# One decoder kernel, its feature mixer: `c` spread by identity products, fewer unread products, two more columns loaded ahead, one engine order into the MLP

## The chip, the cores and the metric

One core of one Trainium2 chip runs the whole program. The metric is the device time in microseconds (us) of one execution; three runs of the kernel before are given, and one more execution was profiled.

## The reference

The reference is a decoder of two layers over 512 tokens of width 1024, all in float32. Layer 0 mixes tokens with a pool mixer, layer 1 with a gated unit; each layer then has an MLP of width 4096 with a squared ReLU. Before every mixer and MLP the activations are normalised, scaled and shifted, and each result is gated; the scales, shifts and gates are `mod = silu(c) @ ada_w + ada_b`, 12288 numbers in all from one vector `c`.

```
c_act = jax.nn.silu(c)
for i in range(DEPTH):
    mod = c_act @ ada_w[i] + ada_b[i]
    sh1, sc1, g1, sh2, sc2, g2 = jnp.split(mod, 6, axis=-1)
    h = modulate(rmsnorm(x, norm_mix_g[i]), sh1, sc1)
    y = pool_mixer(h, ...) if i == 0 else sgu_mixer(h, ...)
    x = x + g1[:, None, :] * y
    h = modulate(rmsnorm(x, norm_mlp_g[i]), sh2, sc2)
    x = x + g2[:, None, :] * jnp.square(jax.nn.relu(h @ mlp_w1[i])) @ mlp_w2[i]
return rmsnorm(x, final_g)
```

The pool mixer takes, in each of four groups of 256 features, the mean over a trailing window of 2, 4, 8 or 16 tokens, subtracts the token itself, and multiplies by a 256x256 matrix.

## The kernel before, in words

**Stages.** The program has a head (layer 0's mixer, about the first 58 us), a sweep (the first 7 of the MLP's 32 column tiles of `w1`, done for all 512 tokens, one 128-row slice `k` of the contraction at a time, eight slices), and then `mlp(0)`, the second mixer and `mlp(1)`. Large products are done as three products of halves: a float32 operand is split into a rounded half `wh` (ScalarE copies it) and a rest `wl` (VectorE subtracts).

**Columns of `mod`.** A *column* is a tile of 128 of `mod`'s numbers, 512 KB of `ada_w`. It is done in one of two ways. On VectorE: one SCALAR_TENSOR_TENSOR over 128x1024 multiplies the tile by `cb`, the vector silu(c) spread over all partitions, and adds up along the row (`column`). On TensorE, for a name that ends in P in `WORK`: eight small products `pt` with silu(c) as the stationary operand, a ScalarE copy `prt`, and one product `pm` with `sel` that adds the four parts (`qm`, `qg`, `qn`). Columns are named `m` (scale and shift of the mixer, group and place), `g` (gate, by 128-feature slice) and `n` (scale and shift of the MLP, by slice `k`).

**`cb`.** `spread_row` loads `c` as a row (`row`, 4 KB), multiplies it by a row of ones in two products of 512 columns (`pc`), and ScalarE copies the result with Silu.

**The order of the head.** Two lists set it. `LOADS` is the order of the transfers on SyncE's queue; its columns go into a ring of 13 slots (three `w4` tiles and five pairs `wh`, `wl`, which the splits use as well), and a load is issued when its slot's last column has been used. `WORK` is the order of the steps, and each step's instructions go to their engines in that order: `sq`, `rms`, `bandr` (squares of tokens, their inverse roots on GpSimd, the window matrix scaled by them), `win` (window products `pq`), `pd` (ScalarE, scale and shift), `pr` (products `po` with `pool_w`), `gf` and `ad` (gate, and VectorE's addition into `xf`), `xt`/`xd` and `bt`/`be` (transposes to features and back), `sm`/`sk`/`ss` (sums of squares), `tot` and `diag` (inverse root of the sums, spread over partitions as `rb`), `hi`/`lo` (split of a sweep weight). `zN` puts N products of `ones` by `ones`, which nothing reads, ahead of the next bank's first product; `SPIN` does it ahead of the sweep.

**The sweep.** For each `k`: VectorE makes `ht`, ScalarE rounds it to `hb`, VectorE subtracts the rest, TensorE does 21 products of 512 columns, and beside them two columns `n` of the next slice and the split of the next weights are done. Columns that `LOADS` does not name are loaded here, into the three `w4` slots alone (`places`). At the slices in `SPILL`, ScalarE issues a transfer of 1 MB that puts half of `x` away to DRAM. The sweep's sums use three banks of the pool `xz` and the four of `ps` (`rb` has the fourth of `xz`).

**Into the MLP.** `mlp(0)` records its instructions and orders them by a cost table. The head's hand order ends with its `with` block, and `mlp` opens another one. The first thing that TensorE does there is the last of the eight columns of `w1`, in `f_run`, in a bank of `ps`.

Of the kernel before, what the change touches and what calls it, by code (L numbers as in the profile page):

```python
# [7 lines left out]
F32 = mybir.dt.float32  # L8
# [6 lines left out]
P = 128  # L15
D = 1024
# [29 lines left out]
def c_g(n, k):  # L46
# [7 lines left out]
    m11 m10 m13 g3 x m12 m33 g2 m31 g7 m30 pw1 m32 m23 m03 pw3 m22 g6 m20 m21 m00 m02 pw2 m01 g5 pw0 g1 g0 g4  # L54
    n01 n00 raw0 n11 raw1
# [3 lines left out]
    z8 rowc z9 z1 m13P qm13 m11 sq2 g3P m10 sq0V edge z9 z7 xt2 sq1V rms0 rms2 xt1 m12 qg3 gf3 sq3V qm10 rms1  # L59
    rms3 qm11 g2 xt3 m33 qm12 fin1 g7 qm33 xd2 qg7 m31 bandr0 xt0 bandr2 xd1 qg2 xd3 gf7 m30 bandr1 qm30 m32  # L60
    qm31 bandr3 xd0 qm32 fin3 win1 win3 m23 gf2 qm23 pd1 pr2 pd3 pr3 ad2 z1 m03P ad3 m22 pr7 qm22 ad7 g6 m20
    bt10 bt11 m21 qg6 qm21 win2 qm20 be10 fin2 gf6 be11 pr6 m00 m02 ad6 qm02 m01 win0 pd2 qm03 qm01 pr4 pr5
    qm00 fin0 g5 qg5 bt31 gf5 sm13 bt30 pd0 ad5 sm11 g1 be31 g0 pr0 qg1 sm12 be30 pr1 sm33 qg0 sm10 sk5 gf0
    ad0 sm30 sm32 g4P sm31 gf1 qg4 ad1 bt01 be01 gf4 ad4 sk4 bt00 be00V sm03 sm02V ss5 sm01V sm00 hi0 s3 ss4
    n01P bt21 tot n00 lo0 be21 bt20 qn00 n11P qn01 z2 diag nf0 qn11 be20
"""

SPIN = 5
EARLY = 2
SPILL = (6, 7)  # L70
# [278 lines left out]
def decoder_kernel(ctx: ExitStack, tc: tile.TileContext, xtok, vecs, rows, fgrow, ada0, ada1, pool_w, w1s, w1, w1f, w1b, w2, w2e, w_v, w_u, w_o, wsT, lnp, bs, out):  # L349
# [3 lines left out]
    ORDERED = {mybir.EngineType.DVE, mybir.EngineType.Activation, mybir.EngineType.SP, mybir.EngineType.Pool}  # L353
# [219 lines left out]

    with (
        tc.tile_pool(name="st", bufs=1) as st,
        tc.tile_pool(name="st2", bufs=2) as st2,
        tc.manual_schedule(engines={mybir.EngineType.DVE, mybir.EngineType.Activation, mybir.EngineType.SP}),
    ):
        row = st.tile([P, D], F32, name="row")
        Y.dma_start(row[0:1], rows[0:1])  # L580


# [69 lines left out]
        def places(name):  # L652

            kind = name.rstrip("0123456789")
            if kind == "n" and int(name[1]) > 1:
                return slots[0:1]
            return [slots[(nslot[0] + j) % len(slots)] for j in range(kind in ("m", "g", "n"))]

        def load(name):
            kind, d = name.rstrip("0123456789"), [int(c) for c in name if c.isdigit()]  # L660
            for j, (pool, tag) in enumerate(places(name)):
# [5 lines left out]
                nslot[0] += kind != "n" or d[0] <= 1  # L667
# [24 lines left out]
        def column(name, out):  # L692
# [132 lines left out]
        wk = {}  # L825
# [71 lines left out]
        def norm_32(k):  # L897
# [5 lines left out]
            rowc=lambda: spread_row(cb, AF.Silu),  # L903
# [15 lines left out]
        for k in range(KD):  # L919
# [54 lines left out]
    def mlp(i, first, extra, last, ending):  # L974
# [3 lines left out]
        with (  # L978
# [45 lines left out]
            def f_run(u, w):  # L1024
                c, f = u
                po = bank("po")
# [419 lines left out]
    mlp(0, first0, ex, gated, ending0)  # L1446

# [184 lines left out]
def _lay_out(inp):  # L1632
# [21 lines left out]
    d["rows"] = f("c")  # L1654
# [48 lines left out]
```

## Time and profile before

| | |
|---|---|
| median of 3 runs | 824.75 us (821.16, 824.84, 824.75) |
| the profiled execution | 825.6 us |
| its span | 823.9 us |
| TensorE (PE) busy | 808.9 us, 98% |
| VectorE (DVE) busy | 689.3 us, 84% |
| ScalarE (ACT) busy | 484.7 us, 59% |
| GpSimd (POOL) busy | 70.4 us, 9% |
| last gate addition of the mixer starts | 50.96 us |
| first `ht` of the sweep starts | 57.97 us |
| first product of the sweep starts | 59.52 us |
| first product of `mlp(0)` starts | 99.08 us |

Rows of the timeline are: start in us, duration in us, engine, line, operation, output<-inputs, shape, count, and in brackets the engine's idle time before it and what ended it. PEld is TensorE's loading of stationary operands. L102 is the helper through which the head's instructions go, L130 the one of `mlp(0)`, so a line number tells little, and the names of tiles do the work. A float32 product shows as two records.

### The profile page before, as it was taken

The page shows a single profiled execution, that of the slowest core. Times are in us where ns is not written, and L with a number is a line of the kernel's source. Part 1 is how long each engine was busy: PE and PEld are TensorE (multiplying, and loading weights), DVE is VectorE, ACT ScalarE, POOL GpSimd, SP SyncE. Part 2 cuts the span into 40 slices and gives each one's busy share as a digit, 9 for nine tenths or more (in the row PEclk, how much of TensorE's full clock was granted, in tenths as well). Part 3 has the DMA queues.
Part 4 walks back from the last instruction along what each step waited for, and adds up shares of the span by engine and source line. Part 5 has one row for each costly group of instructions (what it writes and reads, how often), then busy time and mean ns, then how long its engine had stood idle before and what let it go on. Part 6 is the DMA issues. An engine that isn't in the chain of part 4 may idle for free.

```text
span 823.9 us, 12793 instructions
## 1 busy us (share of the span) xinstructions
PE 808.9 (98%) x4969; PEld 729.9 (89%) x4969; DVE 689.3 (84%) x936; ACT 484.7 (59%) x703; POOL 70.4 (9%) x96
## 2 busy tenths in 40 slices
PE   9999899999999999999999999999999999999996
PEld 7668788999999999888889888989999999999985
DVE  4989878899999999867798967778789988988865
ACT  2576686675766577257333226676766667677522
POOL 3100001010101010001020001000101000111001
PEclk9999999999999999999999999999999999999999
DMA  9969995989988797627856646947888888777402
GB/s 354 411 235 307 364 283 144 271 222 266 228 275 229 247 249 241 200 84 249 277 158 210 220 157 216 325 105 201 192 266 206 258 227 254 186 175 244 140 26 102
DMA packets 43790, 185.47 MB, mean 225 GB/s; under 512 B 4921, under 2 KB 5073, under 8 KB 36434
## 3 DMA queue, kind: packets, MB, share of 16 engines
q1 hardware_dynamic: 35282, 137.72, 46.2%
q0 software_dynamic: 8016, 44.58, 26.9%
q10 hardware_dynamic: 432, 2.36, 0.7%
q8 instruction: 39, 0.64, 0.3%
q14 instruction: 21, 0.17, 0.1%
HBM read 178.34 MB, written 6.30 MB: 224 GB/s over the span
## 4 chain that ended last, share of the span: by engine, by line
PE 86%; DVE 7%; DMA 3%; ACT 2%; issue 1%; POOL 0%; POOLq 0%; DVEq 0%; ACTq 0%
PE po L102 32%; PE pm L130 18%; PE pm L102 17%; PE po L130 15%; DVE ada L102 2%; DVE wl L102 2%; DMA ada<-in_ada 1%; PE px L102 1%; PE pt L102 1%; PE pc L102 1%; DMA raw<-in_w 1%; DVE wh L102 1%; ACT wh L102 1%; PE pq L102 0%; DVE ht L102 0%
## 5 line engine op out<-in xcount | busy, mean ns | idle before, releaser
L102 PE MATMUL po<-hb,wh 128*128 128x256 f32 (+1 forms) x816 | 177.5, 314 | 0.0
L102 PEld LDWEIGHTS po<-hb,wh 128*128 128x128 f32 x816 | 135.1, 191 | 8.5 <-DVE hb L102 0.7
L102 PE MATMUL po<-hb,wl 128*128 128x256 f32 (+1 forms) x408 | 128.8, 316 | 0.7 <-ACT hb L102 0.7
L102 DVE TENSOR_TENSOR wl<-raw,wh 128x1024 fp32r<-128x1024 f32 (+2 forms) x85 | 99.2, 1171 | 26.9 <-ACT wh L102 26.6
L102 ACT ACTIVATE wh<-raw 128x1024 fp32r<-128x1024 f32 (+2 forms) x85 | 85.7, 1017 | 52.8 <-PE pm L102 21.8
L102 PEld LDWEIGHTS po<-hb,wl 128*128 128x128 f32 x408 | 77.9, 191 | 5.6 <-ACT hb L102 1.3
L130 ACT ACTIVATE wh<-raw 128x1024 fp32r<-128x1024 f32 x48 | 50.8, 1060 | 54.4 <-PE pm L130 19.7
L130 PE MATMUL po<-hb,wh 128*128 128x256 f32 (+1 forms) x400 | 78.1, 296 | 0.0
L102 DVE SCALAR_TENSOR_TENSOR ada<-ada,cb 128x1024 f32<-128x1024 f32 x50 | 60.6, 1220 | 12.7 <-DMA ada<-in_ada 7.3
L130 DVE TENSOR_TENSOR wl<-raw,wh 128x1024 fp32r<-128x1024 f32 x48 | 58.5, 1222 | 9.3 <-ACT wh L130 9.0
L130 PEld LDWEIGHTS po<-hb,wh 128*128 128x128 f32 x400 | 63.7, 191 | 2.0
L102 PE MATMUL pm<-wh,oh 128*128 128x512 f32 x188 | 63.8, 357 | 0.0
L130 PE MATMUL pm<-wh,oh 128*128 128x512 f32 x188 | 63.8, 357 | 0.0
L102 PE MATMUL pm<-wh,ol 128*128 128x512 f32 x168 | 63.7, 379 | 0.0
L130 PE MATMUL pm<-wh,ol 128*128 128x512 f32 x168 | 63.7, 379 | 0.0
L130 PE MATMUL pm<-wl,oh 128*128 128x512 f32 x168 | 63.7, 379 | 0.0
L102 PE MATMUL pm<-wl,oh 128*128 128x512 f32 x168 | 63.7, 379 | 0.0
L130 PE MATMUL po<-hb,wl 128*128 128x256 f32 (+1 forms) x201 | 59.4, 296 | 2.0 <-ACT g L130 2.0
L102 PE MATMUL po<-as,wh 128*128 128x256 f32 x288 | 49.0, 275 | 0.0
L102 PEld LDWEIGHTS po<-as,wh 128*128 128x128 f32 x288 | 43.7, 192 | 0.0
L130 PEld LDWEIGHTS po<-hb,wl 128*128 128x128 f32 x201 | 38.4, 191 | 3.4 <-ACT g L130 2.4
L130 PE MATMUL po<-as,wh 128*128 128x256 f32 x240 | 40.8, 275 | 0.0
(275 smaller groups left out, 1886.9 us busy)
## 6 DMA issues: line engine op xcount, KB each, us to landing
ada<-in_ada SPq DMA_DIRECT2D x76, 512.0 KB, 4.6
raw<-in_w1b SPq DMA_DIRECT2D x44, 512.0 KB, 6.2
b<-in_w SPq DMA_DIRECT2D x18, 1024.0 KB, 6.8
bt<-in_w POOLq DMA_DIRECT2D x18, 1024.0 KB, 8.8
raw<-in_w1b POOLq DMA_DIRECT2D x22, 512.0 KB, 6.4
raw<-in_w2e SPq DMA_DIRECT2D x16, 512.0 KB, 3.7
bt<-in_w SPq DMA_DIRECT2D x6, 1024.0 KB, 8.7
b<-in_w POOLq DMA_DIRECT2D x6, 1024.0 KB, 10.4
```

The lines of the kernel that those rows point to most:

```text
L102: return f(*a, **kw)
L130: self.ops.append((name, attr, lambda: f(*a, **kw), out, ins, kw))
```

## The change

`spread_row` no longer loads a row: for each of the eight slices of silu(c), one product with that slice broadcast over 128 columns as the stationary operand and the identity as the moving one. The TensorE columns take the same broadcast in place of the copy `cab`. `WORK` and `LOADS` are other lists: eight TensorE columns (m20 m00 m13 g3 g6 n01 n00 n21) in place of six (m13 g3 m03 g4 n01 n11), the tokens `x` loaded after two columns in place of four, groups 0, 1, 2 summed by token and group 3 by feature, 19 unread products in place of 37, and `n21` and `n10` in the ring's list. `held` marks the ring slots that the sweep's splits take, and a column in `LOADS` takes a ring slot whatever its slice. `SPIN` is 3 in place of 5, `SPILL` is (5, 7) in place of (6, 7). The hand order stays open until `mlp(0)` has been written out, and `mlp(0)`'s first product takes its bank from `xz`.

```diff
 LOADS = """
-    m11 m10 m13 g3 x m12 m33 g2 m31 g7 m30 pw1 m32 m23 m03 pw3 m22 g6 m20 m21 m00 m02 pw2 m01 g5 pw0 g1 g0 g4
-    n01 n00 raw0 n11 raw1
+    m00 m20 x m02 m01 m13 m10 m03 g0 g1 pw0 m12 m11 g2 g3 m23 pw1 m22 m21 m30 pw2 m31 m33 m32 g4 g5 pw3 g6 g7
+    n00 raw0 n01 n21 n11 n10 raw1
 """
 WORK = """
-    z8 rowc z9 z1 m13P qm13 m11 sq2 g3P m10 sq0V edge z9 z7 xt2 sq1V rms0 rms2 xt1 m12 qg3 gf3 sq3V qm10 rms1
+    z5 rowc edge sq0 z2 m20P sq3 z9 z2 xt3 sq2 sq1V rms0 rms2 xd3 m00P xt2 rms3 rms1 m02 bandr0 xd2 z1 m13P
...
-SPIN = 5
+SPIN = 3
-SPILL = (6, 7)
+SPILL = (5, 7)
...
-    ORDERED = {mybir.EngineType.DVE, mybir.EngineType.Activation, mybir.EngineType.SP, mybir.EngineType.Pool}
+    ORDERED = {mybir.EngineType.Pool}
...
+    ordered = ExitStack()
+    ordered.enter_context(tc.manual_schedule(engines={mybir.EngineType.DVE, mybir.EngineType.Activation, mybir.EngineType.SP}))
     with (
         tc.tile_pool(name="st", bufs=1) as st,
         tc.tile_pool(name="st2", bufs=2) as st2,
-        tc.manual_schedule(engines={mybir.EngineType.DVE, mybir.EngineType.Activation, mybir.EngineType.SP}),
     ):
-        row = st.tile([P, D], F32, name="row")
-        Y.dma_start(row[0:1], rows[0:1])
...
-        def spread_row(o, f):
+        def spread_row(o):
             for n in range(2):
                 pc = bank("pc")
-                T.matmul(pc, ones[0:1, :], row[0:1, S * n : S * n + S], start=True, stop=True)
-                A.activation(o[:, S * n : S * n + S], pc, f)
-
-        cab = st.tile([P, KD, 32], F32, name="cab")
-        V.tensor_copy(cab, ca.unsqueeze(2).to_broadcast([P, KD, 32]))
+                for q in range(4):
+                    k = 4 * n + q
+                    T.matmul(pc[:, P * q : P * q + P], ca[:, k : k + 1].to_broadcast([P, P]), ident, start=(q == 0), stop=(q == 3), skip_group_check=True)
+                A.activation(o[:, S * n : S * n + S], pc, AF.Copy)
...
-            if kind == "n" and int(name[1]) > 1:
+            if kind == "n" and name not in LOADS:
                 return slots[0:1]
...
-                T.matmul(pt[q : q + 32], cab[:, k], r[:, k], start=(k < 4), stop=(k >= 4), tile_position=(0, q), skip_group_check=True)
+                T.matmul(pt[q : q + 32], ca[:, k : k + 1].to_broadcast([P, 32]), r[:, k], start=(k < 4), stop=(k >= 4), tile_position=(0, q), skip_group_check=True)
...
+            held[k] = [(tag, len(taken[tag])) for tag in ("wh", "wl")]
+            for tag, _ in held[k]:
+                taken[tag].append(False)
...
+            for tag, n in held[k]:
+                taken[tag][n] = True
...
-                po = bank("po")
+                po = bank("po", xz if i == 0 and u == (0, SWEEP) else None)
...
     mlp(0, first0, ex, gated, ending0)
+    ordered.close()
```

Three places show how the instructions move. The first is VectorE (DVE) at the sweep's last slice: `ht` and `hb` are its operands, `ada,pmv` is the first column of layer 1, and `xf` and `wl<-raw` belong to `mlp(0)`.

```order
 L102 TENSOR_TENSOR wl<-raw,wh 128x896
 L102 SCALAR_TENSOR_TENSOR ht<-xf,scl_92,rb 128x512
-L130 SCALAR_TENSOR_TENSOR ada,pmv<-ada,cb 128x1024
 L102 SCALAR_TENSOR_TENSOR hb<-ht,mods_89,hb 128x512
+L130 SCALAR_TENSOR_TENSOR ada,pmv<-ada,cb 128x1024
 L130 TENSOR_TENSOR xf<-xf 128x4x256
 L130 TENSOR_TENSOR wl<-raw,wh 128x1024 x3
```

The column of layer 1 stood between `ht` and the rest `hb` of the last slice; now it stands behind `hb`.

The second is VectorE in the sweep's second slice (`k` = 1), where the rows `ada,pm` are the columns `n` of the next slice.

```order
 L102 SCALAR_TENSOR_TENSOR ht<-xf,scl_92,rb 128x512
-L102 SCALAR_TENSOR_TENSOR ada,pm_711<-ada,cb 128x1024
+L102 SCALAR_TENSOR_TENSOR ada,pm_628<-ada,cb 128x1024
 L102 SCALAR_TENSOR_TENSOR hb<-ht,mods_89,hb 128x512
-L102 SCALAR_TENSOR_TENSOR ada,pm_711<-ada,cb 128x1024
 L102 TENSOR_TENSOR wl<-raw,wh 128x896
 L102 SCALAR_TENSOR_TENSOR ht<-xf,scl_92,rb 128x512
```

One of its two columns goes (n21, now a TensorE column ahead of the sweep); the other slices keep theirs.

The third is TensorE at the program's start: `pc` is the spread of `c`, `pt` and `pm` are TensorE columns, rows with `ones` as the only input are unread products.

```order
-L102 MATMUL pc<-ones 128x128 x8
-L102 MATMUL pc<-row,ones 128x512 x2
-L102 MATMUL pt<-ones 128x128 x10
-L102 MATMUL pt<-ada,cab 32x128 x8
-L102 MATMUL pm<-sel,prt 128x1
-L102 MATMUL pt<-wh,cab 32x128 x8
-L102 MATMUL px<-ones 128x128 x16
+L102 MATMUL pc<-ones 128x128 x5
+L102 MATMUL pc<-ident,ca 128x128 x8
+L102 MATMUL pt<-ones 128x128 x2
+L102 MATMUL pt<-ada,ca 32x128 x8
+L102 MATMUL px<-ones 128x128 x11
```

Two long one-row products give way to eight of 128 columns, and of the 34 unread products in these rows 18 are left; the transposes `px` of the tokens follow in both.

More of the change, by code (lines that the diff above doesn't have):

```diff
@@ L348, in decoder_kernel @@
 @with_exitstack
-def decoder_kernel(ctx: ExitStack, tc: tile.TileContext, xtok, vecs, rows, fgrow, ada0, ada1, pool_w, w1s, w1, w1f, w1b, w2, w2e, w_v, w_u, w_o, wsT, lnp, bs, out):
+def decoder_kernel(ctx: ExitStack, tc: tile.TileContext, xtok, vecs, fgrow, ada0, ada1, pool_w, w1s, w1, w1f, w1b, w2, w2e, w_v, w_u, w_o, wsT, lnp, bs, out):
     nc = tc.nc
@@ L666, in load @@
                 taken[tag].append(False)
-                nslot[0] += kind != "n" or d[0] <= 1
+                nslot[0] += kind != "n" or name in LOADS
             if kind == "x":
@@ L823, in backed @@
                 V.tensor_copy(o, b)
-        wk = {}
+        wk, held = {}, {}
         pm2 = {}
```

15 lines of the change are left out of this document (7 added, 8 removed).

## The prediction

> **What bounds the kernel now.** I read the chain of waits first, then the stages, then the timeline where a stage left a question. From the start of `mlp(0)` on it is TensorE alone, one group behind the other:
>
> ```profile
> 114.90 5.18 PE pm L130 x25
> 120.08 5.18 PE po L130 x24
> ```
>
> 24 products of 512 columns take 5.18 us, 0.216 each, with nothing between groups, and so it goes on for most of the span. The change touches none of that work, so it can only move the moment at which this stream begins. What lies ahead of it I read by stages, with the busy time of PE, PEld, DVE, ACT and POOL, the granted clock, the DMA engines' share and GB/s:
>
> ```profile
> 20.00:30.00 10.00, 8.96 (x58) 6.99 (x57) 9.33 (x25) 7.36 (x13) 2.73 (x2) 1.00 1.03 408
> 30.00:40.00 10.00, 10.00 (x63) 6.64 (x62) 9.01 (x19) 3.30 (x6) 0.00 (x0) 1.00 1.03 416
> 40.00:50.00 10.00, 9.68 (x52) 5.25 (x50) 9.51 (x21) 7.28 (x24) 0.00 (x0) 1.00 0.98 402
> ```
>
> In the mixer three resources are full at once: TensorE, VectorE, and the DMA engines at some 410 GB/s, so a 512 KB column lands every 1.26 us (0.524 MB by 0.416). Moving work between engines pays there only where all three allow it.
>
> **The mixer**, up to its last gate addition. In the profile it ends at 51.71 (50.96 + 0.75):
>
> ```profile
> 50.96 0.75 DVE L102 SCALAR_TENSOR_TENSOR xf<-po,mg,xf 128x512 f32<-128x512 f32 x1
> ...
> 57.97 0.75 DVE L102 SCALAR_TENSOR_TENSOR ht<-xf,scl,rb 128x512 f32<-128x512 f32 x1 [1.38 <-PE pm L102]
> ```
>
> *Work on VectorE.* Twenty columns become nineteen up to that point, and three whole squares of tokens become one; each is one pass over 1024 elements, about 1.15 from start to start, so 3.45 less. The copy `cab` goes too. *Data.* The list brings the same 24 columns, tokens and `pool_w`, about 30 units of 512 KB, so the last gate lands when it landed before, less one issue slot of SyncE (the row of `c`, 0.37). Before, that column was issued at 35.30, and such columns took 10.0 to land at the median, a little less late in the list, so about 44.5; now 44.1.
>
> ```profile
> 35.30 0.33 SPq L102 DMA_DIRECT2D wl<-in_ada  x1
> ```
>
> ```profile
> wl<-in_ada SPq DMA_DIRECT2D x10, 512.0 KB, 10.0
> ```
>
> The tokens are units 3 to 6 in place of 5 to 8: 2.5 + 0.4 earlier.
>
> ```profile
> L102 SPq DMA_DIRECT2D x<-in_xtok x4: 449/456/478, 3.4 to 5.0; - x4
> ```
>
> ```profile
> DMA to landing us min/median/max: 7.0/7.8/8.6
> ```
>
> Landing ran from 3.4 + 7.0 = 10.4 to about 5.0 + 8.6, and a unit later at the worst, 14.3; now the last token tile is there by about 11.4. *The windows* need the window matrix scaled by four inverse roots. Now ScalarE squares two tiles behind that landing (two passes of about 1.2, to 13.9), GpSimd does four roots, and ScalarE three `bandr` and four `xf` copies behind the last:
>
> ```profile
> 22.07 2.73 POOL L102 TENSOR_TENSOR r<-v,mhalf 128x1 f32<-128x1 f32 x2 [4.25 <-DVE v L102]
> ```
>
> ```profile
> 24.83 0.78 ACT L102 ACTIVATE bandr<-band,r 128x576 f32<-128x576 f32 x1 [0.37 <-POOL r L102]
> 25.51 1.07 ACT L102 ACTIVATE xf<-px 128x512 f32<-128x512 f32 x2
> ```
>
> Before, the last `bandr` ended at 25.6. Now: 13.9 + 4 x 1.15 = 18.5, + 3 x 0.75 + 4 x 0.54 = 22.9. From there I lay out TensorE's stretch from the rows of the same work:
>
> ```profile
> 34.55 1.04 PE L102 MATMUL px<-ident,xf 128*128 128x128 f32 x8
> 35.42 2.08 PE L102 MATMUL pq<-bandr,x 128*128 128x144 f32 x16
> 37.34 1.88 PE L102 MATMUL po<-pd,pw 128*128 128x512 f32 x4
> ```
>
> From start to start a window group takes 1.92 and a `po` pair 1.72. Group 0's last windows end at 23.4; then come three window groups 5.8, eight products 13.8, two TensorE columns with their sums about 1.9, five half transposes about 2.4, and some 0.1 at each of eight changes of producer: 24.7, so the last product ends at 48.1 and the last addition at 48.1 + 0.15 + 0.75 = 49.0. VectorE's own list, followed against the landings, has its next to last pair added by about 45 and the last gate's column done by 46.3, so TensorE is what ends last, no longer VectorE, which trailed the last product by 2.6. **Term: 51.7 to 49.0, -2.7.** Ends: if TensorE were no limit, landing 44.1, one column and two gates with their additions (1.9) give 47.1, -4.6; if the roots come as late as before, 0.
>
> **To `ht`**, the sweep's first, it took 6.26 more (57.97 - 51.71). The same chain of copy, squares, sum, root on GpSimd, `diag` and `rb` stands there. n11 replaces n00 on VectorE and falls into the 1.38 it idled ahead of `ht`; one more copy back (0.69) lies beside the root. TensorE has three columns in place of two between the sums and `rb`, 0.6 more, of which half shows. **Term: +0.3** (0 to +0.9).
>
> **The sweep.** Each slice from the third on is a chain of VectorE alone:
>
> ```profile
> 66.15 0.66 DVE ht L102
> 66.80 0.98 DVE ada L102
> 67.95 0.67 DVE hb L102
> 68.61 1.14 DVE ada L102 x2
> 69.76 1.00 DVE wl L102
> ```
>
> From 66.15 to 70.76 it takes 4.61, while TensorE's 21 products take 21 x 0.216 = 4.53. The column taken out of `k` = 1 is worth 1.15 to VectorE, but not to the sweep: TensorE then becomes the bound. All 168 products need 36.3. Before, from the first at 59.52 to the end of the last at 96.88 it was 37.36:
>
> ```profile
> 90.51 0.74 DVE L102 SCALAR_TENSOR_TENSOR ht<-xf,scl,rb 128x512 f32<-128x512 f32 x1
> 91.17 1.22 DVE L130 SCALAR_TENSOR_TENSOR ada<-ada,cb 128x1024 f32<-128x1024 f32 x1
> 92.31 0.08 DVE L130 DVE_READ_ACCUMULATOR ada<-ada,cb 128x1 f32 x1
> 92.31 0.75 DVE L102 SCALAR_TENSOR_TENSOR hb<-ht,mods,hb 128x512 fp32r<-128x512 f32 x1
> ```
>
> Here layer 1's column delays the last `hb` by 1.14, and it now stands behind. With both edits VectorE reaches the last `ht` about 30.0 (two slices with one column 3.47, five with two 4.61) + 1.2 (the waits for late columns below) after the first, TensorE the last slice 33.5 after it, so only a wait of about 0.3 in the first slice stays. **Term: -0.8** (0 to -1.1).
>
> The columns still come into three slots and still wait for data:
>
> ```profile
> L102 DVE SCALAR_TENSOR_TENSOR ada<-ada,cb 128x1024 f32<-128x1024 f32 x13 | 15.9, 1223 | 1.2 <-DMA ada<-in_ada 1.2
> ```
>
> n20's load now waits for n21's slot, which TensorE reads some 4.4 after the mixer ends, and SyncE's next loads queue behind it; it is wanted some 10 after. A second spill (1 MB, 2.5 us of the DMA engines) also moves into the sweep. Both fall on VectorE's new margin of about 2 over TensorE.
>
> **Into the MLP.** The gap is plain:
>
> ```profile
> 96.45 0.59 PE L102 MATMUL po<-hb,wh 128*128 128x512 f32 x2
> 99.08 0.49 PE L130 MATMUL po<-hb,wl 128*128 128x256 f32 x2 [2.03 <-ACT g L130]
> ```
>
> ```profile
> 96.54 1.06 ACT L130 ACTIVATE wh<-raw 128x1024 fp32r<-128x1024 f32 x1 [2.03 <-DMA raw<-in_w]
> 97.51 1.04 ACT L130 ACTIVATE as<-xf 128x1024 fp32r<-128x1024 f32 x1
> 98.45 1.06 ACT L130 ACTIVATE g<-po 128x512 f32<-128x512 f32 x2
> ```
>
> TensorE waits for a `ps` bank, whose reader `g` stands on ScalarE behind a split that waits for data. With the bank of `rb`, last read by the last `ht`, the wait goes; the weights of the first product are split by about two us before the sweep ends. What is late next is the second column's bank, wanted 5.2 later, and then `p`'s weights:
>
> ```profile
> 106.99 1.22 DVE L130 TENSOR_TENSOR wl<-bt,wh 128x1024 fp32r<-128x1024 f32 x1
> ```
>
> They were ready at 108.2 for a start at 114.9, so 2.2 can be given back and 4 stay. **Term: 99.08 - 96.88 = -2.2** (-1 to -2.2).
>
> **Other edits.** `cb` from identity products is ready earlier, but VectorE's first column now lands only at about 12.7: nothing. The 18 unread products hid in waits: nothing, unless the clock falls (below).
>
> **Sum:** -2.7 + 0.3 - 0.8 - 2.2 = -5.4. The profiled execution took 825.6 (span 823.9, the rest around it), which gives 820.2; the median of the runs shown, 824.75, lies 0.85 lower, so I say 819.4.
>
> **The clock.** Unread products bought clock at the start:
>
> ```profile
> 4.83 3.78 PE L102 MATMUL pc<-row,ones 1*128 1x512 f32 x4
> 8.54 4.43 PE L102 MATMUL pt<-ones 128*128 128x128 f32 x20
> ...
> 14.83 3.84 PE L102 MATMUL px<-ones 128*128 128x128 f32 x32
> ```
>
> The same record takes 0.22 in the second row and 0.12 in the third, while the granted clock reads 1.00 throughout: the array ran at half rate for the first 13 us. In my layout TensorE is about half idle from 12.7 to 21.2, its longest gap 2.4. [...] No row here shows a gap of that kind.
>
> **Rivals.** One row for the last of them:
>
> ```profile
> DVE mg L102 <- PE pm L102: 3.7, 1, 3.7
> ```
>
>  *(a) The clock falls in the thinned stretch* and comes back after the 4.4 us of dense work that the second row above took: half of it is lost, +2.2, 821.6; if the roots are late as well, 823. [...] *(b) Slower: the clock stays at half through the mixer,* since its work comes in pieces. Then the 24.7 us of TensorE's stretch double, and at 844 it is far slower; it turns slower by 0.5% (828.9, so 9.5 to lose) once half rate lasts for over 19 us. Against it: before, the stretch ran at full rate with waits in it. *(c) TensorE is not the mixer's bound,* the pieces overlap better and the landings decide: -4.6 in place of -2.7, 817.5. *(d) The change doesn't do what it says:* a new wait in the mixer (each engine takes its list in order, and before one gate that waited for TensorE held VectorE for 3.7) eats the mixer's term, and the terms behind the mixer stay: 822.
>
> **Chances.** Forecast 0.48 (817.5 to 821.5), (a) 0.15, (b) 0.07, (c) 0.12, (d) 0.18. A measurement of this kernel can tell about 0.5%, 4.1 us, from no change: faster means below 820.6. The forecast's band gives 0.38 of its 0.48 there, (c) all of its 0.12, (d) and (a) some 0.05 of theirs: 0.55. Slower: (b) and a tail of (d), 0.09. The range leaves out (b) and the tail beyond (c): 815.8 to 824.5.
>
> **What would show it.** Right: the last addition near 49, the first `ht` near 55.4, the sweep's products without a gap behind its first slice, `mlp(0)`'s first product right behind the sweep's last, the chain dense from there. Wrong: products `po<-pd` with pairs over 1.72, VectorE waiting for `po` or columns for long in the mixer, columns landing late in the sweep, or a gap of TensorE among the first groups of `mlp(0)` that gives the 2.2 back.

## The result, and the profile after

| | before | changed |
|---|---|---|
| median (20 executions each) | 823.58 us (820.69 to 825.91) | 819.02 us (818.47 to 822.02) |
| the profiled execution | 825.6 us | 821.9 us |
| last gate addition starts | 50.96 | 49.83 |
| first `ht` of the sweep starts | 57.97 | 56.73 |
| first product of the sweep starts | 59.52 | 58.28 |
| first product of `mlp(0)` starts | 99.08 | 94.83 |
| first product of the second mixer starts | 371.16 | 366.82 |
| first `pm` product of `mlp(1)` starts | 558.09 | 554.41 |

The ratio is 0.9954, with a 95% interval of 0.9942 to 0.9965: 4.56 us less by the medians, where 5.4 was forecast. The 824.75 that the forecast started from was the median of three executions; that of twenty is 823.58. The profiled execution is an unlucky one of the changed kernel (821.9, where the median is 819.0), and its profile tells why.

The end of the mixer and the start of the sweep, on VectorE, in the changed kernel:

```profile
49.83 0.75 DVE L102 SCALAR_TENSOR_TENSOR xf<-po,mg,xf 128x512 f32<-128x512 f32 x1 [0.70 <-PE po L102]
...
56.73 0.75 DVE L102 SCALAR_TENSOR_TENSOR ht<-xf,scl,rb 128x512 f32<-128x512 f32 x1 [0.58 <-PE pm L102]
```

VectorE now waits for TensorE ahead of the last addition, as the prediction had it, but the addition comes only 1.13 earlier. From it to the first `ht` little has changed: 6.15 from the addition's end, where it took 6.26. On TensorE, the sweep's first and last products and `mlp(0)`'s first:

```profile
58.28 0.48 PE L102 MATMUL po<-hb,wl 128*128 128x512 f32 x1 [0.78 <-ACT hb L102]
...
94.40 0.59 PE L102 MATMUL po<-hb,wh 128*128 128x512 f32 x2
94.83 0.39 PE L130 MATMUL po<-hb,wl 128*128 128x256 f32 x2
```

The gap of 2.03 is gone: there is no bracket on the last row. From the sweep's first product to its end it is 94.83 - 58.28 = 36.55, where it was 37.36. From the last addition to `mlp(0)`'s first product it takes 45.00 (94.83 - 49.83) where it took 48.12. The chain of waits shows nothing but TensorE from here on:

```profile
58.28 36.71 PE po L102 x168
95.00 15.55 PE po L130 x73
110.55 5.18 PE pm L130 x25
115.73 5.18 PE po L130 x24
```

The lead at the start of the second mixer is 4.34; at the first `pm` of `mlp(1)` it is 3.68. In between lie the same instructions, and they take 187.59 here and 186.93 before; in the experiments below they take 185.9 to 188.0, so these 0.66 are a difference between executions.

**What is new in the mixer.** TensorE from the first products with `pool_w` on, in the same execution:

```profile
23.65 3.70 PE L102 MATMUL po<-pd,pw 128*128 128x512 f32 x8
27.19 0.28 PE L102 MATMUL pm<-sel,prt 128*128 128x1 f32 x2
28.19 0.64 PE L102 MATMUL pt<-wl,ca 128*32 128x128 f32 x16 [0.73 <-DMA wl<-in_ada]
29.22 0.38 PE L102 MATMUL pm<-sel,prt 128*128 128x1 f32 x2 [0.39 <-ACT prt L102]
30.29 1.97 PE L102 MATMUL px<-ident,xf 128*128 128x128 f32 x8 [0.69 <-DVE xf L102]
32.05 4.42 PE L102 MATMUL po<-pd,pw 128*128 128x512 f32 x8
```

Eight records `po<-pd` take 3.70 in the first row and 4.42 in the last; eight `px` take 1.97. Three waits stand between. The windows (busy PE, PEld, DVE, ACT and POOL, granted clock, DMA share, GB/s) show what they led to:

```profile
26.84:30.25 3.41, 1.65 (x22) 1.00 (x20) 3.22 (x10) 1.76 (x4) 0.00 (x0) 1.00 1.01 406
30.00:30.50 0.50, 0.21 (x1) 0.21 (x2) 0.50 (x2) 0.00 (x0) 0.00 (x0) 0.79 1.00 410
33.50:34.00 0.50, 0.50 (x2) 0.19 (x1) 0.29 (x2) 0.00 (x0) 0.00 (x0) 0.80 1.12 442
```

A mean of 0.79 in the second window is 1.00 that becomes 0.50 at 30.29, and 0.80 in the third is 0.50 that becomes 1.00 at 33.70. The clock was halved for 3.41 us, behind a stretch of the same length in which TensorE was busy for 1.65. The early part differs too:

```profile
3.42 3.37 PE L102 MATMUL pc<-ident,ca 128*128 128x128 f32 x16
...
7.74 2.72 PE L102 MATMUL px<-ones 128*128 128x128 f32 x22
```

3.37 for 16 records is half rate (0.21), 2.72 for 22 is full rate (0.12). The full rate is there at about 6.4; in the kernel before, whose unread products still took 0.22 each at 8.54, it came at 12.7.

### The profile page after: what moved, and what is told of

Its sections match the earlier page's. It is cut to its first block, busy times and chain, and to the rows that moved or that the text cites. A ratio compares the mean times of both kernels' runs of the same rounds, so it can differ in the third digit from the quotient of the medians.

```text
span 820.2 us, 12807 instructions
## 1 busy us (share of the span) xinstructions
PE 804.4 (98%) x4977; PEld 727.5 (89%) x4977; DVE 684.4 (83%) x928; ACT 486.6 (59%) x710; POOL 67.9 (8%) x96
## 3 DMA queue, kind: packets, MB, share of 16 engines
q0 software_dynamic: 8016, 44.58, 27.2%
## 4 chain that ended last, share of the span: by engine, by line
PE 80%; DVE 8%; DMA 6%; ACT 3%; issue 1%; SPq 0%; POOL 0%; POOLq 0%; ACTq 0%; DVEq 0%
PE po L102 28%; PE pm L130 18%; PE pm L102 18%; PE po L130 15%; DMA ada<-in_ada 3%; DVE wl L102 2%; DVE ada L102 2%; DMA wh<-in_ada 1%; DVE v L102 1%; ACT wh L102 1%; DMA raw<-in_w_v 1%; DMA raw<-in_w_o 1%; PE px L102 1%; ACT hb L102 1%; PE pq L102 0%
## 5 line engine op out<-in xcount | busy, mean ns | idle before, releaser
L102 PEld LDWEIGHTS po<-hb,wl 128*128 128x128 f32 x408 | 77.9, 191 | 5.9 <-ACT hb L102 1.0
L102 ACT ACTIVATE g<-g 128x512 f32<-128x512 f32 x50 | 31.5, 630 | 14.8 <-DVE g L102 14.1
```

The lines of the kernel that those rows point to most:

```text
L102: return f(*a, **kw)
```

## The experiments

The theory after the result: the handover and the sweep do what was forecast, and the mixer loses about 1.7 to a clock that falls by chance. The rivals: VectorE or the data bounds the mixer whatever the clock does; and, against the prediction's own account, not the lists but the early clock moves the mixer. The table has all medians, with the times that the profile of one execution gives. *Full rate from* is the start of TensorE's first records that follow at 0.11 in place of 0.21; for the one-row products of 512 columns, it is 0.43 in place of 0.85.

| kernel | median, executions | ratio to before, 95% interval | full rate from | last addition | first `ht` | `mlp(0)` |
|---|---|---|---|---|---|---|
| before | 823.58, 20 | | 12.7 | 50.96 | 57.97 | 99.08 |
| changed | 819.02, 20 | 0.9954, 0.9942 to 0.9965 | 6.4 | 49.83 | 56.73 | 94.83 |
| e1, waits filled | 819.15, 9 | 0.9946, 0.9929 to 0.9963 | 5.3 | 47.95 | 54.85 | 92.96 |
| e2, bank of `ps` | 822.44, 12 | 0.9985, 0.9968 to 1.0003 | 5.1 | 47.45 | 54.35 | 94.02 |
| e3, row spread | 819.01, 10 | 0.9948, 0.9930 to 0.9967 | 13.6 | 47.60 | 54.51 | 92.61 |
| e4, before + handover | 820.14, 12 | 0.9963, 0.9944 to 0.9982 | 5.5 | 48.23 | 55.24 | 93.35 |
| e5, before + identity | 821.83, 12 | 0.9982, 0.9966 to 0.9997 | 7.0 | 47.46 | 54.46 | 94.79 |
| e6, before + open order | 823.94, 12 | 1.0008, 0.9991 to 1.0025 | 13.5 | 51.29 | 58.30 | 98.87 |
| e7, before + `xz` bank | 821.65, 12 | 0.9973, 0.9956 to 0.9990 | 13.3 | 51.22 | 58.23 | 96.92 |
| e8, no unread products | 819.24, 7 | 0.9948, 0.9928 to 0.9969 | 16.2 | 47.09 | 53.99 | 93.79 |
| e9, changed, again | 819.53, 12 | 0.9956, 0.9935 to 0.9977 | 5.9 | 47.82 | 54.72 | 92.83 |
| e10, before + both | 819.56, 12 | 0.9948, 0.9929 to 0.9966 | 6.8 | 48.45 | 55.46 | 94.46 |
| e11, fewer unread | 818.64, 10 | 0.9942, 0.9921 to 0.9962 | 8.5 at the latest, then again 18.4 | 48.38 | 55.28 | 93.39 |
| e12, one-row unread | 830.19, 7 | 1.0085, 1.0058 to 1.0111 | 28.5 | 57.16 | 64.19 | 104.76 |

e1 to e4, e5 to e8 and e9 to e12 ran on one chip each, with the kernel before beside them (medians 823.97, 823.81 and 823.49).

**e1, the waits filled.** In the changed kernel's `WORK`:

```diff
-... qg2 qm20 g3P gf0 ad0 qg3 m23 qm23 bt01 bt00 gf3
+... qg2 qm20 z3 g3P gf0 ad0 z1 qg3 m23 qm23 z3 bt01 bt00 gf3
```

> Changed kernel, plus seven unread products in the three waits of TensorE between 27.2 and 30.3 us (three ahead of g3's products, one ahead of its sum, three ahead of the back transposes). Theory, the clock: the granted clock of 0.50 that the changed kernel shows from 30.2 to 33.7 comes from these waits and costs 1.75; here it stays 1.00, the eight records of po<-pd behind it take about 3.6 in place of 4.42, the last gate addition starts near 48.3 to 48.6 in place of 49.83, and the time falls by 1.2 to 1.5 against the changed kernel's 819.0. Rival, VectorE: the clock stays 1.00, but VectorE, which has no wait from 36.5 to 47.4, sets the end; last addition not before 49.5, time within 0.4 of 819.0. Rival, the waits are not the cause: the clock falls all the same.

VectorE's last addition:

```profile
47.95 0.75 DVE L102 SCALAR_TENSOR_TENSOR xf<-po,mg,xf 128x512 f32<-128x512 f32 x1 [0.69 <-PE po L102]
```

The clock stays at 1.00 and the addition is 1.9 earlier than in the changed kernel's first profile, but the median is the same. The nine executions only spread less: 818.78 to 820.22, where the changed kernel's twenty had 818.47 to 822.02. So what was removed is not in the typical execution.

**e2, `mlp(0)`'s first bank from `ps` again.**

```diff
-                po = bank("po", xz if i == 0 and u == (0, SWEEP) else None)
+                po = bank("po")
```

> Changed kernel with mlp(0)'s first product in a bank of ps again, as before. Theory: TensorE waits for the first g on ScalarE, which starts at 96.6 and ends at 97.1, while the sweep's last product is over at 95.0: a gap of 2.0 to 2.3 ahead of mlp(0)'s first product, and 821.0 to 821.3 in place of 819.0. Rival: the open order already moved g ahead, or the slack behind gives the gap back: gap under 0.5 or time within 0.5 of 819.0.

TensorE's first product of `mlp(0)`:

```profile
94.02 0.49 PE L130 MATMUL po<-hb,wl 128*128 128x256 f32 x2 [1.39 <-ACT g L130]
```

The wait for `g` comes back, shorter in this execution than expected. The median is 3.4 above the changed kernel, more than the gap explains, and the executions spread from 819.75 to 825.55. A part of that spread is told by e6.

The same execution answers a question of e1: it has the changed kernel's mixer, no filled waits, a granted clock of 1.00 all through the mixer, and its last addition at 47.45.

**e3, `c` spread from a row again.**

```diff
-                for q in range(4):
-                    k = 4 * n + q
-                    T.matmul(pc[:, P * q : P * q + P], ca[:, k : k + 1].to_broadcast([P, P]), ident, ...)
-                A.activation(o[:, S * n : S * n + S], pc, AF.Copy)
+                T.matmul(pc, ones[0:1, :], row[0:1, S * n : S * n + S], start=True, stop=True)
+                A.activation(o[:, S * n : S * n + S], pc, f)
```

> Changed kernel with c spread again from a loaded row by two one-row products of 512 columns. Theory of the prediction (other edits: nothing): within 0.5 of 819.0, since VectorE's first column stands at 14.05 and cb would be there by about 9.5. Rival, the early clock: the changed kernel's records of unread and identity products fall from 0.21 to 0.11 apart at 6.4 us, those of the kernel before only at 12.7, behind the one-row products; with the row spread TensorE stays at half rate to about 12.7, the transposes of the tokens end 2 to 3 later, the windows start near 21 to 22 in place of 18.85, and the time rises by 1 to 3.

TensorE's unread products ahead of the transposes, and VectorE's last addition:

```profile
9.43 4.72 PE L102 MATMUL px<-ones 128*128 128x128 f32 x22
```

```profile
47.60 0.75 DVE L102 SCALAR_TENSOR_TENSOR xf<-po,mg,xf 128x512 f32<-128x512 f32 x1 [0.69 <-PE po L102]
```

Both sides had a half of it right. TensorE is at half rate to 13.6 (4.72 for 22 records, where the changed kernel took 2.72), and it costs nothing: the windows start 1.3 later than in the changed kernel's profile (20.18 against 18.85), and the end of the mixer is the same as in e2 (47.60 against 47.45). In the changed order the early clock is not on the path: ahead of the windows VectorE waits for data, ScalarE and GpSimd, and not for TensorE.

**e4, the handover alone.** The kernel before with:

```diff
+    ordered = ExitStack()
+    ordered.enter_context(tc.manual_schedule(engines={...DVE, ...Activation, ...SP}))
...
-                po = bank("po")
+                po = bank("po", xz if i == 0 and u == (0, SWEEP) else None)
...
     mlp(0, first0, ex, gated, ending0)
+    ordered.close()
```

> Kernel before with two edits alone: the hand order stays open through mlp(0), and mlp(0)'s first product takes its bank from xz. Theory: the gap of 2.03 ahead of mlp(0)'s first product goes and the last hb of the sweep is 1.1 earlier: first product of mlp(0) at 96.3 to 96.9 in place of 99.08, time 2.2 to 2.8 below the kernel before. Rival: the handover's wait is for the split that waits for data, and stays: under 0.6 below the kernel before.

On TensorE the one-row products, the sweep's first and `mlp(0)`'s first product, and on VectorE the last addition:

```profile
4.83 2.13 PE L102 MATMUL pc<-row,ones 1*128 1x512 f32 x4
...
56.80 0.48 PE L102 MATMUL po<-hb,wl 128*128 128x512 f32 x1 [0.34 <-ACT hb L102]
...
93.35 0.38 PE L130 MATMUL po<-hb,wl 128*128 128x256 f32 x2
```

```profile
48.23 0.75 DVE L102 SCALAR_TENSOR_TENSOR xf<-po,mg,xf 128x512 f32<-128x512 f32 x1
```

By the medians it is 3.8 less than the kernel before beside it, where 2.2 to 2.8 were expected. From the last addition to `mlp(0)` it takes 45.12, against 48.12 before and 45.00 in the changed kernel: the two edits give all of the handover and the sweep. The sweep takes 36.55 from its first product, as in the changed kernel, although this kernel still does two columns at `k` = 1. The expected start of `mlp(0)` was missed by 3, and the first row says why: the four one-row products took 3.78 in the profile of before and take 2.13 here. The program's instructions up to there are the same; in this execution the full rate came at 5.5, and the last addition is 2.7 earlier. In the kernel before the full rate comes early or late by chance (5.5 here; 12.7, 13.5 and 13.3 with the same start in the profile of before, e6 and e7), and its profile shows a late one. How that reaches the mixer's end is seen on VectorE, at the gate of its first TensorE column for gates (g3), in the kernel before and in e4:

```profile
20.57 0.22 DVE L102 SCALAR_TENSOR_TENSOR mg<-pm,vec 128x1 f32<-128x1 f32 x1 [3.68 <-PE pm L102]
```

```profile
17.83 0.21 DVE L102 SCALAR_TENSOR_TENSOR mg<-pm,vec 128x1 f32<-128x1 f32 x1
```

The sum `pm` stands on TensorE behind the unread products and transposes. At half rate it comes late and VectorE stands idle for 3.68; in e4 it waits for data instead and finds the sum ready. From this gate to the last addition it takes 30.4 in both, and also in e6 (20.89 to 51.29) and e7 (20.82 to 51.22), so what is lost here is lost at the mixer's end.

**e5, the identity spread alone.** The kernel before with the change's `spread_row`, without the row and without `cab`:

```diff
-        Y.dma_start(row[0:1], rows[0:1])
...
-                T.matmul(pc, ones[0:1, :], row[0:1, S * n : S * n + S], start=True, stop=True)
+                for q in range(4):
+                    T.matmul(pc[:, P * q : P * q + P], ca[:, k : k + 1].to_broadcast([P, P]), ident, ...)
```

> Kernel before with one edit alone: c spread by identity products (no row load, ca in place of cab). Theory, the early clock: TensorE's records go from 0.21 to 0.11 apart at 12.7 us in the profile of the kernel before, whose four one-row products of 512 columns lie in between, and at about 5.2 us in the handover experiment, which runs the same instructions there; with full products in their place the change comes by 8.5 us in every execution, the last gate addition stands near 48.2 as in the handover experiment (50.96 in the profile of before), and the median falls by 1 to 2.5 with the fastest runs near 820.5. Rival, the prediction (other edits: nothing; the changed kernel with the row spread is no slower): within 0.6 of the kernel before.

```profile
7.55 2.40 PE L102 MATMUL pt<-ones 128*128 128x128 f32 x20
...
94.79 0.49 PE L130 MATMUL po<-hb,wl 128*128 128x256 f32 x2 [1.47 <-ACT g L130]
```

```profile
47.46 0.75 DVE L102 SCALAR_TENSOR_TENSOR xf<-po,mg,xf 128x512 f32<-128x512 f32 x1
```

The first row (TensorE) is full rate, 0.12 a record where the kernel before's same products took 0.22; the last one (VectorE) has the mixer's end at 47.46, 3.5 earlier than in the profile of before and no later than with the change's lists. The ratio excludes no change, narrowly.

**e6 and e7, the handover's two edits apart.** e6 has e4's order without the bank, e7 the bank without the order.

> Kernel before with the hand order open through mlp(0) alone; mlp(0)'s first product stays in a bank of ps. Theory: layer 1's column moves behind the last hb, the sweep takes 38.1 from the first ht to mlp(0) or to the gap in place of 38.9 (0.8 less), and the gap of TensorE ahead of mlp(0) stays at 2 or grows, since the split that waits for data lands no earlier: 0 to 0.8 below the kernel before. Rival: the order alone brings most of the handover experiment's 3 to 4: over 2 below.

> Kernel before with mlp(0)'s first bank from xz alone; the hand order ends where it did. Theory: the gap of 2.03 goes, the column of layer 1 still delays the last hb: 2.0 to 2.5 below the kernel before, mlp(0)'s first product 38.9 behind the first ht. Rival: without the open order the first product waits for something else: under 1 below.

TensorE at `mlp(0)`'s start, e6 and then e7:

```profile
98.87 0.80 PE L130 MATMUL po<-hb,wl 128*128 128x256 f32 x2 [2.30 <-ACT g L130]
99.46 1.06 PE L130 MATMUL po<-hb,wh 128*128 128x512 f32 x2
...
102.72 0.59 PE L130 MATMUL po<-hb,wh 128*128 128x512 f32 x2
```

```profile
96.92 0.38 PE L130 MATMUL po<-hb,wl 128*128 128x256 f32 x2
```

e7 is as expected: the gap goes, 2.2 below the kernel before by the medians. e6 is worth nothing that can be measured. Its sweep is shorter (36.55), but the gap stays, and behind it the same pair of products takes 1.06 at 99.46 and 0.59 at 102.72: the granted clock was 0.50 from 98.7 to 102.1, and the first group of `mlp(0)` to the first `pm` took 17.24 in place of 15.55. So behind this gap of 2.30 another 1.7 was lost, half of the 3.4 us for which the clock was halved.

**e8, no unread products at all.** The changed kernel with all `z` steps taken out of `WORK` and:

```diff
-SPIN = 3
+SPIN = 0
```

> Changed kernel without any unread product (all z steps out, SPIN 0). Theory of the prediction's rival (b): the unread products hold the clock; without them TensorE's work of the first 20 us comes in pieces, the records stay at half rate into the windows (24 us and later), and the time rises by 3 to 10 against 819.0. Rival: the identity products and the transposes are enough, or the half rate costs nothing ahead of the windows (in the row spread experiment TensorE was at half rate to 14.0 and the time was the same): within 1 of 819.0.

TensorE's transposes of the tokens, and VectorE's last addition:

```profile
13.68 1.97 PE L102 MATMUL px<-ident,x 128*128 128x128 f32 x8
```

```profile
47.09 0.75 DVE L102 SCALAR_TENSOR_TENSOR xf<-po,mg,xf 128x512 f32<-128x512 f32 x1 [0.69 <-PE po L102]
```

Half rate to 16.2, and the earliest end of the mixer of all. The rival held: in the changed order the half rate ahead of the windows was free (last addition 47.09, against 47.45 in e2 with full rate from 5.1), and the early unread products buy nothing that can be measured. Those ahead of the sweep may have bought something in this execution: the clock fell at 57.1 for 3.4 us, and from the sweep's first product to `mlp(0)` it took 38.24 in place of 36.55. TensorE had been busy for 1.85 of the 3.41 us ahead of the fall; in the changed kernel, with its three unread products there, the thinnest stretch of that length has 2.58 (54.87 to 58.28). The median (819.24) doesn't show it.

**e9, the changed kernel once more.** No edit.

> The changed kernel once more, unchanged. Theory, a clock that falls by chance: the waits of TensorE between 27.2 and 30.3 stand in every execution (the ps bank, row spread and no unread products experiments show them too), but the granted clock fell there only in the one that was profiled first; so more likely than not it reads 1.00 from 26 to 40 here, the last gate addition starts at 47.3 to 48.0 in place of 49.83, and the execution is near 818.8. Rival: the fall belongs to this kernel, last addition near 49.8 and granted clock 0.5 near 30 to 34 again. Median 819.0 either way.

TensorE where the clock had fallen, and VectorE's last addition:

```profile
29.94 1.09 PE L102 MATMUL px<-ident,xf 128*128 128x128 f32 x8 [0.69 <-DVE xf L102]
30.87 3.60 PE L102 MATMUL po<-pd,pw 128*128 128x512 f32 x8
```

```profile
47.82 0.75 DVE L102 SCALAR_TENSOR_TENSOR xf<-po,mg,xf 128x512 f32<-128x512 f32 x1 [0.61 <-PE po L102]
```

The same wait of 0.69 stands there, but the clock stays: 1.09 in place of 1.97 and 3.60 in place of 4.42, 1.7 in all, and the last addition is 2.0 earlier. The fall is chance, not a property of the kernel: with the same instructions it came in one profiled execution and not in the other.

**e10, the kernel before with e4's and e5's edits,** so the change without its lists, the edits to the ring that go with them, `SPIN` and `SPILL`.

> Kernel before, its lists kept, with the handover's two edits and the identity spread. Theory: with these two the changed kernel's gain is complete and the new lists add nothing: last gate addition near 47.5 (47.46 with the identity spread alone), mlp(0)'s first product near 92.6, time within 0.6 of the changed kernel (819.0 to 819.6). Rival, the prediction's mixer term: the lists take work off VectorE and let groups start earlier, worth another 1 to 2.7: 820.0 to 821.7 here.

VectorE's last addition and its one wait in the sweep, and TensorE's wait there and `mlp(0)`'s first product:

```profile
48.45 0.75 DVE L102 SCALAR_TENSOR_TENSOR xf<-po,mg,xf 128x512 f32<-128x512 f32 x1
...
76.78 1.23 DVE L102 SCALAR_TENSOR_TENSOR ada<-ada,cb 128x1024 f32<-128x1024 f32 x1 [1.44 <-DMA ada<-in_ada]
```

```profile
80.48 0.48 PE L102 MATMUL po<-hb,wl 128*128 128x512 f32 x1 [0.35 <-ACT hb L102]
...
94.46 0.38 PE L130 MATMUL po<-hb,wl 128*128 128x256 f32 x2
```

819.56, against 819.53 for the changed kernel beside it: the new lists add nothing that can be measured. The two times expected were missed: the mixer ended 1.0 later than in e5, which has the same lists, and the sweep was longer. The second row shows the latter. A column came 1.44 late, VectorE with two columns in every slice but the first had no margin for it, and TensorE waited: 37.44 for the sweep in place of 36.55. That is this execution's; e4, with the same lists, took 36.55.

**e11, a version from the experiments:** the changed kernel without the early unread products, with two later ones and a longer `SPIN`.

```diff
-... ad0 qg3 m23 qm23 bt01
+... ad0 z1 qg3 m23 qm23 z1 bt01
...
-SPIN = 3
+SPIN = 5
```

> Changed kernel without the unread products of the first 26 us, with one ahead of g3's sum and one ahead of the back transposes, and five in place of three ahead of the sweep. Theory: without the early ones the last gate addition stands near 47.1 to 47.3 as without any (47.09), and with the late ones the clock does not fall in the sweep's first slice as it did there at 57.1: 818.1 to 818.7, 0.3 to 0.9 below the changed kernel. Rival: executions differ by more than that, no difference from 819.0 that shows.

VectorE's last addition:

```profile
48.38 0.75 DVE L102 SCALAR_TENSOR_TENSOR xf<-po,mg,xf 128x512 f32<-128x512 f32 x1 [0.70 <-PE po L102]
```

TensorE at the first and the last tile of the tokens, and the windows ahead of a fall of the clock and behind it:

```profile
8.51 0.33 PE L102 MATMUL px<-ident,x 128*128 128x128 f32 x1 [0.65 <-DMA x<-in_xtok]
...
12.32 1.33 PE L102 MATMUL px<-ident,x 128*128 128x128 f32 x5 [0.93 <-DMA x<-in_xtok]
```

```profile
8.10:11.51 3.41, 0.98 (x3) 0.41 (x3) 1.30 (x3) 1.31 (x3) 0.36 (x1) 1.00 1.03 422
11.51:14.93 3.42, 2.60 (x23) 1.86 (x24) 0.20 (x4) 2.53 (x5) 0.19 (x1) 0.50 1.03 420
```

It has the lowest median, 0.9 below the changed kernel beside it, but the intervals of the two lie on each other, so it is not shown to be faster. The last addition was not where it was expected: 48.38 is 1.3 later than in e8, and the windows started at 20.73 in place of 19.26. Two things differ. TensorE was at full rate at 8.51 (0.33 for a single record that takes 0.48 at half rate, at 7.99 in e8), then waited for the tiles one by one, and the granted clock was 0.50 from 11.51 to 18.34. And the last tile came at 12.32, where it came at 11.41 in e8; that alone is 0.91 of the 1.47 by which the windows are later. So it isn't shown how late the full rate may come for nothing.

**e12, one-row unread products.** The kernel before with:

```diff
-            T.matmul(o[:, 0:P], ones, ones, start=True, stop=True)
+            T.matmul(o[:, 0:P], ones[0:1, :], ones[0:1, :], start=True, stop=True)
```

> Kernel before with its unread products made one-row products (one row of ones by one row of ones, same 128 columns, same number and time). Theory: products that use one row of the array do not bring the clock up: TensorE's records stay 0.21 apart through z8, the row products, z10 and z16 to the transposes of the tokens near 22 us, full rate not before 24, and the windows, the last gate addition and the end come 2 to 5 later than in the kernel before's slow start (last addition 53 to 56). Rival: only the time that TensorE is busy counts: full rate by 13 as before, time within 0.7 of the kernel before.

TensorE's unread products and the transposes behind them, VectorE's last addition, and a window ahead of the sweep:

```profile
15.52 7.19 PE L102 MATMUL px<-ones 1*128 1x128 f32 x32
22.64 3.67 PE L102 MATMUL px<-ident,x 128*128 128x128 f32 x16
```

```profile
57.16 0.75 DVE L102 SCALAR_TENSOR_TENSOR xf<-po,mg,xf 128x512 f32<-128x512 f32 x1
```

```profile
62.60:66.00 3.40, 3.15 (x25) 2.83 (x24) 2.01 (x5) 2.87 (x9) 0.00 (x0) 1.00 0.74 258
```

As the theory had it, and larger than it said: TensorE is busy from 1.1 to 22.6 with hardly a pause and stays at half rate; the full rate comes at 28.5, in the course of the transposes of the tokens, which use all rows. The last addition is 6.2 later than in the profile of before, and the median 6.7 above the kernel before. The last row has the same thing at the other end: TensorE busy for 3.15 of 3.40, but with full products for only 1.5, the rest being one-row unread ones, and the granted clock fell at 66.0. At the mixer's gate of e4's rows VectorE waited 9.42 for `pm` here.

## Why the prediction was right, and where it was not

The time came out as forecast (819.02 for 819.4), in part by luck: the base of 824.75 lay 1.2 above the median of twenty executions, and the change was 0.8 less than the 5.4 forecast. The two terms behind the mixer held. The mixer's term rests on a step that failed, and how much of the 4.6 the mixer gives in a typical execution is not settled.

- **Into the MLP, -2.2:** held. The gap is gone (first product 94.83, right behind the sweep), and nothing of it came back among the first groups; e7 alone, the bank, is 2.2 below the kernel before. That the clock can also halve behind such a gap (e6: a gap of 2.30, then 0.50 for 3.4 us and 1.7 lost) was not in the term. The edit is then worth more in some executions than in others (behind the gap of 2.03 in the profile of before the granted clock stayed at 1.00), and that may be why the medians of e2 and of e4 move by more than one profile's gap. An estimate from the falls below: if idle time of 1.5 in a stretch of 3.41 halves the clock (the fall behind 1.85 busy in e8, none behind 1.95 in e5), a gap of 2.03 does so in 2.4 of 3.41 positions of the stretch (3.41 + 2.03 - 2 x 1.5), about 0.7 of the executions if all positions are equally likely.
- **The sweep, -0.8:** the size held (37.36 to 36.55). Of its two edits, layer 1's column behind `hb` does it alone (e4: 36.55 with both columns at `k` = 1); the column taken out of `k` = 1 is a margin, which counts when data come late (e10, 0.9).
- **To `ht`, +0.3:** measured -0.1. The third TensorE column hid.
- **The mixer, -2.7 by less work on VectorE, earlier tokens and a dense TensorE:** in the profiled execution -1.13; in the changed kernel's second one -3.1. The step that failed is the sentence on the other edits, which gave the identity spread and the unread products nothing because VectorE's first column lands at 12.7 anyway. It looked at `cb` and not at the clock. In three of the four profiled executions with the old start (before, e6, e7) TensorE stays at half rate to about 13, the sum `pm` of g3 is late by it, and VectorE waits 3.3 to 3.7 for that sum; in the fourth (e4) the full rate is early and there is no such wait. That was the mixer's price: with the identity spread and the old lists it ends with an addition at 47.46 and 48.45 (e5, e10), with the new lists at 47.09 to 48.38 when the clock does not fall in the windows or behind them (e1, e2, e3, e8, e9, e11). The new lists do not measurably add to that. They are another way to the same gain: with them a late full rate cost nothing (47.60 in e3 and 47.09 in e8), with the old ones it cost 2.8 to 3.8 (e6 and e7 against e5 and e10). The prediction had both rows in it: 4.43 for twenty unread products against 3.84 for thirty-two, read as the price of the first 13 us, and the gate that waited 3.7 for `pm`, used only as an example for rival (d). Its layout of the changed mixer was near, with two misses that nearly cancel: in e9 group 0's last windows end at 21.9 in place of 23.4, and TensorE needs 25.9 from there in place of 24.7. What it was set against, 51.7, was a late start; with e4's early one the old lists end at 48.98.
- **Rival (a), the clock falls,** came true in the execution that was profiled, at 30.3 and not between 12.7 and 21.2, at about the price that it gave (1.7 by the rows and 2.0 at the last addition, for +2.2; 821.9 for 821.6). The forecast's sum has nothing for the clock. That gaps like those of its layout, the longest 2.4, leave the clock up is shown by no run: in the profiled execution it fell behind 3.41 us in which TensorE was busy for 1.65 and waited for 0.73 at the longest. The fall is not in the typical execution. **Rival (b)** is out: even without unread products the clock comes up ahead of the windows (16.2 and 19.26, e8). **(c)** is out, since VectorE waits 0.6 to 0.7 for TensorE ahead of the last addition in every profile of the changed mixer. **(d)** is small: TensorE's three waits between 27.2 and 30.3 are 1.8 in all, the first of them for a column's data.

By parts, against the kernel before on the same chip: the handover 3.8 less by the medians (its interval reaches from 1.5 to 4.6), the identity spread 2.0 (0.2 to 2.8), both together 3.9 (2.8 to 5.8), the whole change 4.6 (2.9 to 4.8). The parts do not add up: on top of the handover the identity spread is worth 0.1 and the whole change 0.7, where the spread alone is worth 2.0. The intervals are too wide to say whether they should. So by the medians the mixer's share lies anywhere from nothing to 2.8, and the 3 of the profiles is against late starts. The kernel before's spread (820.7 to 828.0 over all its executions) seems to have both causes: the executions lie within 4.3 and 5.4 with the gap closed and the old start (e7, e4), 4.2 with the identity spread and the gap (e5), and 2.8 with the gap closed and the identity spread (e10). Which execution had which stays open, since only one of each was profiled.

## What to carry to other kernels

Before a schedule is rearranged, see whether the same instruction takes the same time in all of its rows; if it takes double in some (0.213 from record to record against 0.112 here), the clock is a term of the sum, and one profile shows one draw of it. Where unread work is meant to bring TensorE's clock up, try how much of the array it has to use: here 128 rows had the full rate at 12.7, one row at 28.5 (e12). A gap like the one of 2.0 to 2.3 here is better closed than moved, since it can be paid for twice (e6, 1.7 on top of 2.30). When an engine waits long for another in the profile, ask what made the other one late: here that row held the price of a late clock. When a change of order and a change of cost aim at the same wait, try each alone: their gains need not add.

## What the runs showed of the hardware

**One-row products did not bring the clock up.** With the same unread products on one row in place of 128, the full rate came at 28.5 in place of 12.7 (e12), and TensorE at 93% busy by the profile, half of it with one-row products, did not keep it (62.6 to 66.0).

**With the same instructions the full rate came at 5.5 to 13.5.** It came at 12.7, 13.5 and 13.3 in the kernel before, e6 and e7, and at 5.5 in e4; with full products in place of the one-row ones it was 5.1 to 7.0 in six executions (the changed kernel, e1, e2, e5, e9 and e10). In four executions the fall lies a whole number of steps of 3.41 behind the rise to full rate: 7 in the changed kernel (from 6.40 to 30.29), 11 in e12 (28.5 to 66.0), 12 in e8 (16.2 to 57.1), 25 in e6 (13.5 to 98.7). The falls lasted 3.41 in the changed kernel, 3.4 in e6 and e8, and 6.83, twice as long, in e11. Counted back from the rise in such steps, the stretch ahead of e4's rise goes from 2.0 to 5.4 and has 0.6 of one-row products at its end, while the one from 2.4 to 5.8 in the profile of before has 1.0 of them and brought no rise, and neither did the next one there, with 2.8 of them. An estimate from these rows: the kernel before offers 3.7 us ahead of its one-row products (1.12 to 4.83), so a stretch of 3.41 with at most 0.6 to 1.0 outside them finds room there in 1.5 to 2.3 of 3.41 positions (0.3 + 2 x 0.6 to 0.3 + 2 x 1.0), about half of the executions if all positions are equally likely.

**The falls needed no idle stretch.** Laid out in these steps, the stretches ahead of the falls had TensorE busy for 0.98 (e11), 1.27 (e6), 1.61 (changed kernel, 26.88 to 30.29) and 1.85 (e8) of 3.41, and 3.15 in e12, half of it with one-row products; those with 1.95 (e5) and 2.06 (e9) brought none. The nearest two, e8's with a fall and e5's without:

```profile
53.73:57.14 3.41, 1.85 (x11) 1.34 (x9) 3.15 (x5) 2.83 (x8) 0.00 (x0) 1.00 0.97 336
```

```profile
92.26:95.68 3.42, 1.95 (x10) 1.42 (x10) 2.82 (x4) 3.42 (x6) 0.00 (x0) 1.00 1.02 398
```

Where a thin stretch lies seems to matter as well: in the kernel before TensorE was busy for 1.45 of the 3.40 us from 95.60 to 99.00, which is not one of its steps, and the granted clock stayed at 1.00.

**The granted clock of the profile read 1.00 while TensorE still ran at half rate at the start** (0.213 from record to record up to 12.5 in the kernel before and up to 6.4 in the changed kernel, against 0.112 later). In these traces it shows a fall and the return from it, but not the first rise; the time of one record does.
